# RWKV-7 and gMLP trunk: k, r, v and g projections by single channel tiles, with hi and lo activations side by side in one 512-column product

## The chip, the cores and the metric

The kernel runs on one core of a Trainium2 chip. The metric is device microseconds for one execution; smaller is better. A core has a matrix engine (TensorE, PE in the profile), three engines that work on tiles (VectorE is DVE, ScalarE is ACT, GpSimd is POOL), and SyncE (SP), which here issues most DMA transfers.

## The reference

Two residual layers over 256 tokens of width 2048, then a final RMS norm. All inputs are float32. Layer 0, where the change lies, projects the normalised input `z` to 4 x 4096 channels (r, k, v and a gate g) and to four low-rank inputs:

```python
def rwkv7_bidir_mixer(h, w_in, mu_prev, mu_next, ...):
    z = h @ w_in
    zs, gate = z[..., :SHIFT_COLS], z[..., SHIFT_COLS:]
    zs = zs + mu_prev * (shift_prev(zs) - zs) + mu_next * (shift_next(zs) - zs)
    r, k, v, dw, da = jnp.split(zs, ...)
    ...                                   # decay, in-context rate, normalised keys kk
    for d, rev in ((0, False), (1, True)):
        y = y + wkv_scan(rh, heads(decay), kd_h, vh, -kk, kk * a_h, rev)
        bonus = bonus + jnp.sum(rh * kd_h * r_k, axis=-1, keepdims=True) * vh
    ...                                   # group norm of y, plus bonus
    return (out * jax.nn.silu(gate)) @ w_out
```

Layer 1 is a gated gMLP: `u`, `v` and a gate from one projection to 3 x 4096 channels, a 128 x 128 spatial mixing per group of 256 channels, and an output projection.

## The kernel before

**Precision by halves.** Weights and activations are float32; each operand is split into hi (rounded to the matmul's fp32r form) and lo (the remainder), and a product is hi·hi + hi·lo + lo·hi. Weights arrive as raw tiles of 128 x 1024 floats (512 KB, two buffers, issued by SP). ACT casts raw to hi (L150) and DVE subtracts to get lo (L151); up to three converted tiles wait ahead of PE (three buffers each of hi and lo). The activations `z` are stored transposed as `zh` and `zl`, 128 channels by 16 k tiles by 256 tokens each.

**The mixer stage.** The 4096 channels are 32 channel tiles of 128, handled as 16 pairs (b). A pass p projects k and r of pair p and v and g of pair p-1, in four segments. A segment (`mains`, L436) fetches four weight tiles of 4 k tiles x 256 columns. For every k tile and each of the two channel tiles, `project` issues three matmuls through `mm3` (L165 to L167), each with 256 moving columns: whi·zh, whi·zl, wlo·zh. Both channel tiles accumulate in the two halves of one PSUM bank (tag "acc", two buffers). Then k, r and v pass through `shifted` (ACT scales by c0, DVE adds the neighbour tokens' shares, all read from PSUM: L395, L396, L398), and g through a tanh and one DVE operation (L450, L451).

**The second layer already has another form.** `project_wide` (L194) works on an interleaved tile `zc` with hi and lo side by side: whi times the 512 columns of hi and lo fills both halves of a bank (L204), wlo times the 256 hi columns adds to the first half (L206). `gated` then copies the second half to SBUF on ACT (L1065) and adds the first half on DVE (L1066).

**What sets the order.** Beside the projections a pass runs, for earlier pairs: low-rank updates (`rates`, tile `up`), the factors of the recurrence (`factors`), gram matrices (`grams`, tile `gp`, masked into `Gs`), a triangular inverse on DVE (`inverses`, L637 and L639, 31 steps), transposes (`bp`, `vp`), the chunk chain (`chain`, tiles `xp`, `uu`, `sp`, `yp`) and `finish`. Each is a generator that yields a due time within a planned pass of `PERIOD` = 78 units; a loop always advances the one that is due first. `mains` yields after each k tile. From this program a scheduler with a simulated timeline lays down each engine's fixed instruction order and the semaphores. Engines execute their own order strictly.

The storage of `zh` and `zl` is used again later for activations of the output projections (`oA` in `early_out`, `pA` in the second layer).

Of the kernel before, what the change touches and what calls it, by code (L numbers as in the profile page):

```python
# [22 lines left out]
def trunk(tc, x, norm_g, final_norm_g, w_in, mu_prev, mu_next, w0, w_up, a0, a_up, k_k, k_a, r_k,  # L23
# [149 lines left out]
    def want_cols(w, c_off, b, name):  # L173
        a = min(KT, 1 << int(math.log2(RAW // b)))
        wv = w.rearrange("(k p) c -> p k c", p=P)
        for k0 in range(0, KT, a):
            want(wv[:, k0:k0 + a, c_off:c_off + b], a, b, f"{name}{k0}")
# [32 lines left out]

    def acc_pair(name):
        return sm(name, "acc").rearrange("p (i t) -> p i t", i=2)
# [69 lines left out]
    zT = (zp.tile([P, KT, T], F32R, tag="zh", name="zh"), zp.tile([P, KT, T], F32R, tag="zl", name="zl"))  # L282
# [73 lines left out]
    for todo in plan:  # L356
        for s, b in todo:
# [3 lines left out]
            else:  # L361
                want_cols(w_in, segment[s] + b * 2 * P, 2 * P, f"w{s}{b}_")
# [27 lines left out]
    def shifted(acc, dst, b, m):  # L390

        for cl in range(2):
            a = acc[:, cl]
            j = m * NCT + 2 * b + cl
            S.activation(dst[:, cl], a, AF.Identity, scale=c0[:, j:j + 1])  # L395
            V.scalar_tensor_tensor(dst[:, cl, 1:], a[:, :T - 1], col["mp"][:, j:j + 1], dst[:, cl, 1:],  # L396
                                   ALU.mult, ALU.add)
            V.scalar_tensor_tensor(dst[:, cl, :T - 1], a[:, 1:], col["mn"][:, j:j + 1], dst[:, cl, :T - 1],  # L398
                                   ALU.mult, ALU.add)
# [36 lines left out]
    def mains(todo, st):  # L436
        slot = dict(k=0, r=4, g=12, v=8) if "k" in dict(todo) else dict(v=0, g=4)
        last = -4
        for s, b in todo:
# [5 lines left out]
            acc = acc_pair(f"acc{s}{b}")  # L445
            for i, _ in enumerate(project(2 * P, [acc[:, 0], acc[:, 1]], zT)):
                yield last * MT + i * dt
            if s == "g":
                SG = fr.tile([P, 2, T], F32, tag="SG", name=f"SG{b}", bufs=2)
                S.activation(SG, acc, AF.Tanh, scale=0.5)  # L450
                V.scalar_tensor_tensor(SG, SG, 1.0, acc, ALU.add, ALU.mult)  # L451
                st[b]["SG"] = SG
            elif s == "v":
                Vt = fr.tile([P, 2, T], F32, tag="Vt", name=f"Vt{b}", bufs=2)
                shifted(acc, Vt, b, 2)
                st[b]["Vt"] = Vt
            else:
                t = fr.tile([P, 2, T], F32, tag=f"{s}t", name=f"{s}t{b}")
                shifted(acc, t, b, dict(r=0, k=1)[s])
# [711 lines left out]
```

## Time and profile before

| | us |
|---|---|
| median of 3 runs | 2230.92 (2229.87 to 2234.58) |
| the profiled execution's own time | 2229.16 |
| its span, first to last instruction | 2227.4 |
| the mixer stage in it (37.9 to 1273.9) | 1236.0 |
| PE busy in the span | 2179.0 |
| DVE busy in the span | 1608.1 |
| ACT busy in the span | 1345.2 |

The span is 1.8 us shorter than the profiled execution's time. Busy time of PE is a union of overlapping matmuls: it tells that PE has work, and not how fast it works. The mean length of one matmul in a row (for example 290 ns) is longer than the distance to the next matmul's start for the same reason. A row that ends in "idle before, releaser" tells how long the engine stood still ahead of such instructions, and which instruction ended the wait.

### The profile page before, as it was taken

To read this page: it belongs to the slowest core of one execution; us is meant where nothing else is said; L and a number is where in the kernel's file an instruction comes from. 1 tells how busy PE (TensorE), PEld (TensorE's weight loads), DVE (VectorE), ACT (ScalarE), POOL (GpSimd) and SP (SyncE) were. 2 spreads that over 40 slices of the span, in tenths; PEclk is the share of its full clock that TensorE was granted. 3 is DMA by queue.
4 is the path that set the end of the run, shared out by engine and by line. 5 is a ranking of instruction groups with operands and counts; after the bars stand their busy time and mean duration, and the time that the engine had idled before them with its cause. 6 is when DMAs were issued, how large, how long until landed. Compare 5 with 4: busy or idle time off the path is not lost.

```text
span 2227.4 us, 48630 instructions
## 1 busy us (share of the span) xinstructions
PE 2179.0 (98%) x19984; PEld 1944.7 (87%) x19984; DVE 1608.1 (72%) x3121; ACT 1345.2 (60%) x2128; POOL 171.8 (8%) x230
## 2 busy tenths in 40 slices
PE   7999999999999999999999999999999999999998
PEld 7889999999999999999999877778888888888886
DVE  5797788787977977887888764465546777777444
ACT  6556777777767676776767664464444444444443
POOL 2210110011001101100010000000000000000000
PEclk9999999999999999999999999999999999999999
DMA  5555444454445544444545555586766666665664
GB/s 167 140 145 142 109 126 134 125 137 112 130 127 143 139 126 131 129 125 136 137 124 138 167 174 177 173 263 189 221 204 190 198 189 195 195 193 192 195 198 154
DMA packets 352687, 356.01 MB, mean 160 GB/s; under 512 B 78160, under 2 KB 300112, under 8 KB 352336
## 3 DMA queue, kind: packets, MB, share of 16 engines
q1 hardware_dynamic: 332208, 331.66, 51.6%
q10 hardware_dynamic: 20256, 21.24, 3.2%
q8 instruction: 157, 2.57, 0.5%
q14 instruction: 66, 0.54, 0.1%
HBM read 329.78 MB, written 6.29 MB: 151 GB/s over the span
## 4 chain that ended last, share of the span: by engine, by line
PE 69%; ACT 10%; DMA 9%; DVE 8%; issue 3%; ACTq 0%; SPq 0%; POOL 0%; POOLq 0%; DVEq 0%
PE uacc L204 5%; PE gacc L204 5%; DMA raw_o<-in_rwkv_w_out_dram 3%; PE oacc L166 3%; PE oacc L167 3%; PE oacc L165 3%; PE gp L584 3%; PE gacc L206 3%; PE uacc L206 3%; PE vacc L167 3%; PE vacc L165 3%; PE vacc L166 3%; ACT Dt L623 2%; PE accv L165 2%; PE accg L167 2%
## 5 line engine op out<-in xcount | busy, mean ns | idle before, releaser
L204 PE MATMUL uacc<-z,whi_u 128*128 128x512 f32 x512 | 179.0, 394 | 0.0
L204 PE MATMUL gacc<-z,whi_g 128*128 128x512 f32 x512 | 177.3, 393 | 0.0
L167 PE MATMUL accg<-zh,wlo_wg 128*128 128x256 f32 x512 | 149.6, 292 | 2.5 <-DVE wlo_wg L151 2.4
L165 PE MATMUL accv<-zh,whi_wv 128*128 128x256 f32 x512 | 149.2, 291 | 1.1 <-ACT whi_wv L150 1.1
L167 PE MATMUL accr<-zh,wlo_wr 128*128 128x256 f32 x512 | 148.7, 290 | 0.6 <-DVE wlo_wr L151 0.5
L165 PE MATMUL acck<-zh,whi_wk 128*128 128x256 f32 x512 | 148.1, 289 | 1.1 <-ACT whi_wk L150 1.1
L165 PE MATMUL accr<-zh,whi_wr 128*128 128x256 f32 x512 | 149.0, 291 | 0.0
L165 PE MATMUL accg<-zh,whi_wg 128*128 128x256 f32 x512 | 148.4, 290 | 0.0
L166 PE MATMUL accr<-zl,whi_wr 128*128 128x256 f32 x512 | 148.1, 289 | 0.0
L167 PE MATMUL accv<-zh,wlo_wv 128*128 128x256 f32 x512 | 147.5, 288 | 0.1
L167 PE MATMUL acck<-zh,wlo_wk 128*128 128x256 f32 x512 | 146.2, 286 | 1.0 <-DVE wlo_wk L151 1.0
L166 PE MATMUL accv<-zl,whi_wv 128*128 128x256 f32 x512 | 147.2, 287 | 0.0
L166 PE MATMUL accg<-zl,whi_wg 128*128 128x256 f32 x512 | 147.0, 287 | 0.0
L166 PE MATMUL acck<-zl,whi_wk 128*128 128x256 f32 x512 | 147.0, 287 | 0.0
L206 PE MATMUL uacc<-z,wlo_u 128*128 128x256 f32 x512 | 142.4, 284 | 0.0
L206 PE MATMUL gacc<-z,wlo_g 128*128 128x256 f32 x512 | 140.2, 279 | 0.0
L151 DVE TENSOR_TENSOR wlo_v<-raw_v,whi_v 128x1024 fp32r<-128x1024 f32 x64 | 78.4, 1225 | 80.4 <-ACT whi_v L150 80.4
L151 DVE TENSOR_TENSOR wlo_o<-raw_o,whi_o 128x1024 fp32r<-128x1024 f32 x64 | 78.2, 1224 | 77.5 <-ACT whi_o L150 77.2
L639 DVE TENSOR_TENSOR X<-X,TD 128x126 f32<-128x126 f32 (+22 forms) x496 | 126.5, 255 | 9.4
L637 DVE TENSOR_TENSOR TD<-La,X 128x126 f32<-128x126 f32 (+22 forms) x496 | 125.6, 253 | 10.6
L151 DVE TENSOR_TENSOR wlo_p<-raw_p,whi_p 128x1024 fp32r<-128x1024 f32 x60 | 73.9, 1232 | 75.7 <-ACT whi_p L150 75.7
L150 ACT CAST whi_p<-raw_p 128x1024 fp32r<-128x1024 f32 x60 | 63.1, 1051 | 91.5 <-PE oacc L167 87.3
(331 smaller groups left out, 6842.3 us busy)
## 6 DMA issues: line engine op xcount, KB each, us to landing
raw_wk<-in_rwkv_w_in_dram SPq DMA_DIRECT2D x64, 512.0 KB, 3.7
raw_wr<-in_rwkv_w_in_dram SPq DMA_DIRECT2D x64, 512.0 KB, 3.7
raw_wv<-in_rwkv_w_in_dram SPq DMA_DIRECT2D x64, 512.0 KB, 3.7
raw_wg<-in_rwkv_w_in_dram SPq DMA_DIRECT2D x64, 512.0 KB, 3.7
raw_o<-in_rwkv_w_out_dram SPq DMA_DIRECT2D x64, 512.0 KB, 4.0
raw_v<-in_gmlp_w_in_dram SPq DMA_DIRECT2D x64, 512.0 KB, 3.7
raw_u<-in_gmlp_w_in_dram SPq DMA_DIRECT2D x64, 512.0 KB, 3.5
raw_g<-in_gmlp_w_in_dram SPq DMA_DIRECT2D x64, 512.0 KB, 3.6
```

Of the source, the lines that this page charges most:

```text
L150: latest[0] = S.copy(hi, raw)
L151: latest[1] = V.tensor_tensor(lo, raw, hi.bitcast(F32), ALU.subtract)
L165: PE.matmul(acc, a[0], b[0], start=first, stop=False, skip_group_check=True)
L166: PE.matmul(acc, a[0], b[1], start=False, stop=False, skip_group_check=True)
L167: PE.matmul(acc, a[1], b[0], start=False, stop=last, skip_group_check=True)
L204: PE.matmul(acc.rearrange("p h t -> p (h t)"), hi[:, j, cs], zc[:, k].rearrange("p h t -> p (h t)"), start=k == 0, stop=False, skip_group_ ...
L206: PE.matmul(acc[:, 0], lo[:, j, cs], zc[:, k, 0], start=False, stop=k == KT - 1, skip_group_check=True)
L584: PE.matmul(gp[h][:, c].rearrange("p q t -> p (q t)"), BK[H[h], d, cl, c].rearrange("p q t -> p (q t)"), AR[H[h], d, cl, c].rearrange("p q ...
L623: S.copy(Dt[r0:r0 + 32].rearrange("p t u -> p u t"), Gs[q * 32:q * 32 + 32, h, :, q * 32:q * 32 + 32])
L637: V.tensor_tensor(tv, La[:, j, 0:j].unsqueeze(2).to_broadcast([P, j, n]), X[:, j:j + 1, m:].to_broadcast([P, j, n]), ALU.mult)
L639: V.tensor_tensor(X[:, 0:j, m:], X[:, 0:j, m:], tv, ALU.add)
```

## The change

The k, r, v and g projections take the second layer's form, one channel tile at a time. A weight tile is now 8 k tiles x 128 columns, so that every contiguous run in memory is 512 bytes instead of 1024, with 512 KB per load as before. `mains` calls `project_wide` for each of the two channel tiles of a segment with a PSUM bank of its own: per k tile one matmul of 512 columns and one of 256. It yields after each k tile of one channel tile, twice as often as before. The eviction copies the lo half to a temporary `pa` (ACT), adds the hi half (DVE), and the shifting or gating reads `pa` instead of PSUM, per channel tile. `zh` and `zl` become two strided views of one interleaved tile, and the later users of that storage get one tile in place of two.

```diff
     def want_cols(w, c_off, b, name):
-        a = min(KT, 1 << int(math.log2(RAW // b)))
+        a = min(KT, RAW // b if b == P else 1 << int(math.log2(RAW // b)))
...
-    zT = (zp.tile([P, KT, T], F32R, tag="zh", name="zh"), zp.tile([P, KT, T], F32R, tag="zl", name="zl"))
+    zi = zp.tile([P, KT, 2, T], F32R, tag="z", name="z0")
+    zT = [zi[:, :, i] for i in range(2)]
...
-                want_cols(w_in, segment[s] + b * 2 * P, 2 * P, f"w{s}{b}_")
+                for cl in range(2):
+                    want_cols(w_in, segment[s] + (2 * b + cl) * P, P, f"w{s}{b}_{cl}")
...
-    def shifted(acc, dst, b, m):
-
-        for cl in range(2):
-            a = acc[:, cl]
-            j = m * NCT + 2 * b + cl
-            S.activation(dst[:, cl], a, AF.Identity, scale=c0[:, j:j + 1])
-            V.scalar_tensor_tensor(dst[:, cl, 1:], a[:, :T - 1], col["mp"][:, j:j + 1], dst[:, cl, 1:],
-                                   ALU.mult, ALU.add)
-            V.scalar_tensor_tensor(dst[:, cl, :T - 1], a[:, 1:], col["mn"][:, j:j + 1], dst[:, cl, :T - 1],
-                                   ALU.mult, ALU.add)
+    def shifted(a, dst, j):
+
+        S.activation(dst, a, AF.Identity, scale=c0[:, j:j + 1])
+        V.scalar_tensor_tensor(dst[:, 1:], a[:, :T - 1], col["mp"][:, j:j + 1], dst[:, 1:], ALU.mult, ALU.add)
+        V.scalar_tensor_tensor(dst[:, :T - 1], a[:, 1:], col["mn"][:, j:j + 1], dst[:, :T - 1], ALU.mult, ALU.add)
...
-            acc = acc_pair(f"acc{s}{b}")
-            for i, _ in enumerate(project(2 * P, [acc[:, 0], acc[:, 1]], zT)):
-                yield last * MT + i * dt
-            if s == "g":
-                SG = fr.tile([P, 2, T], F32, tag="SG", name=f"SG{b}", bufs=2)
-                S.activation(SG, acc, AF.Tanh, scale=0.5)
-                V.scalar_tensor_tensor(SG, SG, 1.0, acc, ALU.add, ALU.mult)
...
+            tag, n = dict(k=("kt", 1), r=("rt", 1), v=("Vt", 2), g=("SG", 2))[s]
+            dst = fr.tile([P, 2, T], F32, tag=tag, name=f"{tag}{b}", bufs=n)
+            for cl in range(2):
+                acc = sm(f"acc{s}{b}_{cl}", "acc").rearrange("p (h t) -> p h t", h=2)
+                for i, _ in enumerate(project_wide(P, [acc], zi)):
+                    yield last * MT + (cl * KT + i) * dt / 2
+
+                a = fr.tile([P, T], F32, tag="pa", name=f"pa{s}{b}_{cl}")
+                S.copy(a, acc[:, 1])
+                V.tensor_tensor(a, acc[:, 0], a, ALU.add)
+                if s == "g":
+                    S.activation(dst[:, cl], a, AF.Tanh, scale=0.5)
+                    V.scalar_tensor_tensor(dst[:, cl], dst[:, cl], 1.0, a, ALU.add, ALU.mult)
+                else:
+                    shifted(a, dst[:, cl], dict(r=0, k=1, v=2)[s] * NCT + 2 * b + cl)
+            st[b][dict(r="Rt", k="Kt", v="Vt", g="SG")[s]] = dst
...
-        oA = [zp.tile([P, HE, T], F32R, tag=t, name=f"{t}_o0") for t in ("zh", "zl")]
+        oA = zp.tile([P, 2, HE, T], F32R, tag="z", name="z_o0")
+        oA = [oA[:, i] for i in range(2)]
...
-    pA = [zp.tile([P, HE, T], F32R, tag=t, name=f"{t}_o1") for t in ("zh", "zl")]
+    pA = zp.tile([P, 2, HE, T], F32R, tag="z", name="z_o1")
+    pA = [pA[:, i] for i in range(2)]
```

More of the change, by code (lines that the diff above doesn't have):

```diff
@@ L209, in project_wide @@
                 yield
-    def acc_pair(name):
-        return sm(name, "acc").rearrange("p (i t) -> p i t", i=2)
     n3 = 3 * NCT
@@ L444, in mains @@
             yield last * MT
-            acc = acc_pair(f"acc{s}{b}")
-            for i, _ in enumerate(project(2 * P, [acc[:, 0], acc[:, 1]], zT)):
-                yield last * MT + i * dt
-            if s == "g":
-                SG = fr.tile([P, 2, T], F32, tag="SG", name=f"SG{b}", bufs=2)
[L450 to L459, printed above, removed]
-                st[b][dict(r="Rt", k="Kt")[s]] = t
+            tag, n = dict(k=("kt", 1), r=("rt", 1), v=("Vt", 2), g=("SG", 2))[s]
[13 more added lines that the diff above has]
+            st[b][dict(r="Rt", k="Kt", v="Vt", g="SG")[s]] = dst
         if ("g", NB - 1) in todo:
```

## The prediction

> **What bounds the kernel now.** I read the page's engine line first, then its chain, then the stretch in which the four projections run.
>
> ```profile
> PE 2179.0 (98%) x19984; PEld 1944.7 (87%) x19984; DVE 1608.1 (72%) x3121; ACT 1345.2 (60%) x2128; POOL 171.8 (8%) x230
> PE 69%; ACT 10%; DMA 9%; DVE 8%; issue 3%; ACTq 0%; SPq 0%; POOL 0%; POOLq 0%; DVEq 0%
> ```
>
> The matrix engine (PE) works 98% of the span, and the chain that ended last runs through it for 69%. The other 31% says that ACT, DVE and the weight loads are never far behind. By stretch (columns: PE, weight load, DVE, ACT, POOL, each with its instructions; clock, DMA share, GB/s):
>
> ```profile
> 37.90:1273.90 1236.00, 1215.05 (x14578) 1135.07 (x14576) 1013.90 (x2321) 868.87 (x1489) 133.37 (x170) 0.99 0.49 133
> 220.00:1260.00 1040.00, 1031.64 (x12844) 959.69 (x12839) 854.86 (x2015) 749.05 (x1297) 104.83 (x136) 1.00 0.49 131
> 794.00:848.90 54.90, 54.76 (x666) 50.98 (x665) 50.41 (x133) 36.34 (x67) 4.02 (x7) 1.00 0.46 126
> ```
>
> The first row is the mixer stage, from the first k product to the last g product; all that changes lies in it. The second is its steady part: PE idles 1040 - 1031.64 = 8.4 us, the granted clock is 1.00, DVE is busy 82%, ACT 72%. So PE sets the pace there. The third row is the crowded part of one pass over a channel pair: DVE is busy 50.41 of 54.90 us (92%).
>
> A busy PE tells nothing of its rate, since matmuls overlap. The rate comes from start to start in the timeline: an unbroken run of k and r products, first and last start, 39 spacings apart; and an unbroken run of the u and g products of the second layer, which already have the form that the change brings, 20 pairs apart (columns: start, us of one, engine, line).
>
> ```profile
> 787.23 0.28 PE L166 MATMUL acck<-zl,whi_wk 128*128 128x256 f32 x1
> ...
> 791.90 0.28 PE L166 MATMUL accr<-zl,whi_wr 128*128 128x256 f32 x1
> ...
> 1749.87 0.39 PE L204 MATMUL uacc<-z,whi_u 128*128 128x512 f32 x1
> 1750.10 0.28 PE L206 MATMUL uacc<-z,wlo_u 128*128 128x256 f32 x1
> ...
> 1756.80 0.39 PE L204 MATMUL gacc<-z,whi_g 128*128 128x512 f32 x1
> ```
>
> One 256-column matmul takes 4.67 / 39 = 0.1197 us, so the three products of one weight tile (hi by hi, hi by lo, lo by hi) take 0.3592 us. The pair of one 512-column and one 256-column matmul takes 6.93 / 20 = 0.3465 us.
>
> **The change part by part.** *The products.* Four segments of 32 channel tiles with 16 k tiles each are 2048 places. Each loses three matmuls of 256 columns and gets one of 512 and one of 256: 0.3592 - 0.3465 = 0.0127 us less, 2048 x 0.0127 = 26.0 us off the path. The rounding of the four starts to 0.01 us allows 2.6 us either way. The columns are the same in number (768); what goes is the overhead of the third matmul.
>
> The Trainium skill ("TensorE: Matmul & The Clock Gate", Back-to-back issue gap) gives for isolated matmuls the columns at the full clock and about 2.5 ns on top. By it, 3 x 109.2 would become 215.8 + 109.2 ns, and 2048 x 2.5 ns are only 5.1 us, an estimate from that page. The two runs above measure 119.7 ns where it has 109.2 and 346.5 where it has 325.0, so the trace has a larger price per matmul, and the measurement decides.
>
> *Cuts.* The run of projections is cut where other products come in. What a cut costs:
>
> ```profile
> 701.40 0.49 PE L584 MATMUL gp<-AR,BK 64*128 64x128 f32 x4
> ...
> 705.91 0.28 PE L165 MATMUL acck<-zh,whi_wk 128*128 128x256 f32 x1
> 706.12 0.69 PE L722 MATMUL uu<-Xs,TTs 128*64 128x64 f32 x16
> 706.74 1.16 PE L584 MATMUL gp<-AR,BK 64*128 64x128 f32 x16
> 707.83 0.39 PE L166 MATMUL acck<-zl,whi_wk 128*128 128x256 f32 x1
> 708.05 0.28 PE L167 MATMUL acck<-zh,wlo_wk 128*128 128x256 f32 x1
> ...
> 710.05 0.69 PE L729 MATMUL sp<-SUV,BT 128*64 128x64 f32 x16
> ...
> 1282.22 0.39 PE L167 MATMUL oacc<-whi_o,rt_o 128*128 128x512 f32 x1
> 1282.54 0.38 PE L713 MATMUL xp<-SUV,Gs 128*64 128x64 f32 x4
> ...
> 1769.29 0.40 PE L204 MATMUL uacc<-z,whi_u 128*128 128x512 f32 x1
> 1769.52 0.38 PE L1095 MATMUL sgu<-wsT,vn_bh 128*128 128x128 f32 x2
> ```
>
> The last matmul before the cut takes 0.21 instead of 0.12, the first behind it 0.22: 0.19 us a cut. A 512-column matmul ahead of a cut takes 0.32 in one row and 0.23 in another, so the price stays about the same. The program hands the projections out in steps half as long, so two kinds of work that shared a cut can now fall into two. The stretch around 706 has such a cut, with uu and gp together. The other cuts nearby begin at 701.40 and 710.05, so there is one about every 4 us and some 300 in the stage. Bounds: no more cuts, or a third more (100 x 0.19 = 19 us). I take 20 more, 4 us, nearer to none since the order of the other work stays.
>
> *Evictions.* Each of the 128 channel tiles gets an ACT copy and a DVE addition, which the second layer already does at the same shape; g's tanh and its product become two of 256 columns instead of one of 512.
>
> ```profile
> L1065 ACT COPY Gt<-uacc 128x256 f32<-128x256 f32 x32 | 12.0, 374 | 16.8 <-PE uacc L206 16.8
> L1066 DVE TENSOR_TENSOR U<-uacc,Gt 128x256 f32<-128x256 f32 x32 | 13.5, 421 | 2.1 <-ACT Gt L1065 0.7
> L450 ACT ACTIVATE SG<-accg 128x512 f32<-128x512 f32 x16 | 9.7, 607 | 0.1
> L481 ACT ACTIVATE TH<-up,pc 128x256 f32<-128x256 f32 x64 | 26.9, 473 | 8.6 <-PE up L167 7.8
> L451 DVE SCALAR_TENSOR_TENSOR SG<-SG,accg 128x512 f32<-128x512 f32 x16 | 10.9, 682 | 9.0 <-ACT SG L450 9.0
> L568 DVE SCALAR_TENSOR_TENSOR BQ<-rt,pc,TH 128x256 f32<-128x256 f32 x32 | 14.1, 469 | 0.0
> L395 ACT ACTIVATE rt<-accr,c 128x256 f32<-128x256 f32 x32 | 15.2, 474 | 12.1 <-DVE rt L398 11.6 <-PE accr L167 0.2
> L396 DVE SCALAR_TENSOR_TENSOR rt<-accr,pc,rt 128x255 f32<-128x255 f32 x32 | 15.3, 479 | 2.6 <-ACT rt L395 2.1
> ```
>
> ACT gets 128 x 0.374 + 16 x (2 x 0.473 - 0.607) = 53.3 us, DVE 128 x 0.421 + 16 x (2 x 0.469 - 0.682) = 58.0 us. The shifting operations now read SBUF instead of PSUM; the 469 ns of L568, whose operands all lie in SBUF, against the 479 of L396 say that this saves nothing worth counting. None of the added time lies on PE's path as long as DVE and ACT keep up: in the stage DVE idles 1236 - 1013.9 = 222.1 us now and 1210 - 1071.9 = 138.1 then (89% busy), ACT 367 now and 288 then. If that cover were gone, all 58 us would be paid. What the cover lets through I size by the steady row: PE idles 8.4 us there while DVE has its present room; with the room down by 222.1 / 138.1 = 1.61 I let the idle grow alike, by 5 us. Bounds: nothing, or 58 us.
>
> The new temporary has one buffer. One tile's eviction is 0.374 + 0.421 + 0.474 + 2 x 0.479 = 2.2 us against 16 x 0.3465 = 5.5 us to fill the next, so it holds nobody up. A new handoff comes with it: on ACT the scaling of a tile queues behind DVE's addition, and behind it wait weight casts. In exchange a handoff goes: L395 waits 11.6 us for L398 in the row above, the second tile's scaling for the first tile's shifts out of the same bank. I set the two equal. A bank is held 0.8 us then, and comes round every 5.5 us.
>
> *Weight loads.* Each load still brings 512 KB but in runs of 512 bytes, 1024 instead of 512. No load of that shape is in the trace; the nearest have 1024 runs of 256 bytes.
>
> ```profile
> raw_wk<-in_rwkv_w_in_dram SPq DMA_DIRECT2D x64, 512.0 KB, 3.7
> RC<-AR SPq DMA_DIRECT2D x32, 256.0 KB, 5.2
> Gs<-AR SPq DMA_DIRECT2D x32, 256.0 KB, 3.7
> L145 SPq DMA_DIRECT2D raw_wk<-in_rwkv_w_in_dram x64: 367/368/1567, 31.1 to 1165.0; - x64
> L684 SPq DMA_DIRECT2D RC<-AR x32: 596/663/1619, 85.5 to 1294.4; - x32
> L150 ACT CAST whi_wk<-raw_wk 128x1024 fp32r<-128x1024 f32 x64 | 67.2, 1051 | 65.7 <-DMA raw_wk<-in_rwkv_w_in_dram 43.4 <-PE accg L166 12.5 <-PE acck L166 5.3
> ACT whi_wk L150 <- DMA raw_wk<-in_rwkv_w_in_dram: 43.4, 21, 5.9
> L151 DVE TENSOR_TENSOR wlo_wk<-raw_wk,whi_wk 128x1024 fp32r<-128x1024 f32 x64 | 78.0, 1220 | 35.2 <-ACT whi_wk L150 34.9 <-PE xp L713 0.2
> ```
>
> Landing is thus between 3.7 and 5.2 us; I take 4.4, the middle, with issue on SP's queue at 0.66 instead of 0.37. The dependent copies of RC and Gs stand on the same queue and go up to 0.3 us later per load. A raw buffer then turns in 0.66 + 4.4 + 1.05 + 1.22 = 7.3 us, and two give a load every 3.7 us; the stage asks for 256 + 16 loads in 1210 us, one every 4.4, with three converted ahead. So the longer landing is hidden behind the converted tiles and costs nothing; if that cover is thin it comes back as the second rival. Bounds of its cost: 0, and what that rival gives.
>
> *At no cost.* The grouping rule of the loads gives 8 k tiles for a 128-column load by the old and the new formula. The hi and lo activations move into one tile of the same bytes, so no instruction is added; the later users of that storage write after the last g product as before.
>
> **The sum.** Against the profiled execution: 2229.16 - 26.0 + 4 + 5 = 2212.2 us. That execution lies 1.76 us below the median of the runs, 2230.92, so the median should be 2213.9; I say 2213.
>
> **The rivals.**
> *DVE takes over as the bound (slower).* Place: the crowded part of a pass (794 to 849), with 4.5 us of DVE idle per pass. Five of a pass's eight additions should fall there, 2.1 us, and the extra handoffs eat more. It decides once PE, three weight tiles ahead, runs out of them. For it: 92% busy there. Against it: PE's waits in the steady part are on ACT, and on DVE there is one of 0.2 us:
>
> ```profile
> PE yp L731 <- ACT SUV L724: 2.8, 4, 1.1
> ...
> PE up L165 <- DVE NK L503: 0.2, 1, 0.2
> ```
>
> If half of the 58 us gets through: 2230.9 - 26 + 4 + 29 = 2238; all of it: 2267.
> *The weight supply falls behind.* For it: ACT already sits waiting for landings, 43.4 us at 21 of the 64 loads of wk. Against it: the 3.7 against 4.4 us above. If a third of the 256 loads is awaited, as wk's are now, each 0.7 us late, 60 us reach ACT; if a third of that gets to PE, 20 us: 2213.9 + 20 = 2234; none, 2214.
> *The isolated rate holds and only 5 us come off.* As a mechanism here: the third matmul's overhead is hidden by the others. 2230.9 - 5 + 9 = 2235. Against it: the two unbroken runs above.
> *No cuts and waits are added and the 512-column matmul hides part of the price of a cut.* For it the 0.23 at 1769.29, against it the 0.32 at 1282.22. 2230.9 - 26 - 150 x 0.09 = 2191, without the last term 2205; so about 2198.
>
> **How the numbers follow.** No change means within 0.2%, 2226.5 to 2235.4; that is about what a measurement of this kernel can tell. Forecast 0.57, at 2203 to 2222; DVE takes over 0.14 (slower); the supply 0.15, of it 0.08 faster and 0.07 same; the isolated rate 0.06 (same); the last 0.08 (faster). Faster 0.73, same 0.13, slower 0.14. The range leaves out most of the DVE case, and the lowest part of the last: 2196 to 2239.
>
> **What would show it.** The spacing of the projections should be 0.23 and 0.12 in turn, 4096 matmuls of k, r, v and g instead of 6144; the stage some 17 us shorter; DVE at 88 to 89% in it and PE's idle in the steady part 10 to 15 us; landings of 4 to 5 us. It would be wrong if PE waits on lo weights, on Gs or on BK for more than 20 us in all, if the pair takes more than 0.352 us, or if the projections are cut much oftener than 300 times.

## The result, and the profile after

The changed kernel takes 2289.69 us (median of 4 runs, 2287.49 to 2294.89), the kernel before on the same chip 2232.52 us (median of 4). The ratio is 1.026, with a 95% interval of 1.0238 to 1.0282: 57 us slower. The prediction said 2213 us, 2196 to 2239, and was wrong in sign.

The page of the changed kernel: busy time by engine, the chain that ended last by engine, and the load of the k weights.

```profile
PE 2194.6 (96%) x17936; PEld 1849.3 (81%) x17936; DVE 1651.5 (72%) x3265; ACT 1387.1 (61%) x2272; POOL 183.2 (8%) x230
PE 62%; DVE 15%; ACT 10%; DMA 9%; issue 4%; POOL 1%; ACTq 0%; POOLq 0%; DVEq 0%; SPq 0%
raw_wk<-in_rwkv_w_in_dram SPq DMA_DIRECT2D x64, 512.0 KB, 3.9
```

PE has 2048 matmuls fewer, as the change says, and yet is busy 15.6 us longer. DVE's part of the chain went from 8% to 15%, PE's from 69% to 62%. A load of wk in 512-byte runs lands in 3.9 us here, where the prediction estimated 4.4 and the longer runs took 3.7.

All of the time lies before the second layer. This is its first weight load on PE (the row gives count, shortest/median/longest in ns, first and last start), before and then after:

```profile
L204 PEld LDWEIGHTS uacc<-z,whi_u x512: 187/187/192, 1672.4 to 2030.5; 128*128 128x128 f32 x171
```

```profile
L204 PEld LDWEIGHTS uacc<-z,whi_u x512: 187/187/192, 1732.7 to 2090.9; 128*128 128x128 f32 x171
```

The second layer starts 60.3 us later, and the spans differ by 60.5 (2227.4 and 2287.9). From that start to the end both kernels take 555 us. By stretch, in the changed kernel (columns as in the prediction), the mixer stage and its steady part:

```profile
37.00:1324.70 1287.70, 1226.81 (x12445) 1035.00 (x12444) 1049.97 (x2441) 909.36 (x1627) 144.57 (x170) 0.96 0.48 127
220.00:1260.00 1040.00, 1000.69 (x10662) 842.80 (x10660) 850.71 (x2027) 749.10 (x1356) 106.53 (x130) 0.97 0.48 125
```

The stage went from 1236.0 to 1287.7 us. PE idles 60.9 us in it where it idled 21.0, and the granted clock is 0.96 instead of 0.99. In the steady part PE idles 39.3 us, not 8.4. DVE is the row to look at: it was busy 854.86 of 1040 us before and is busy 850.71 now, though it has more to do. Its share did not rise to fill the idle time. The work was stretched to the share that it already had.

The products did become shorter. The timeline shows an unbroken run of g's products, first and last start, 16 pairs apart:

```profile
1260.18 0.40 PE L204 MATMUL accg<-z,whi_wg 128*128 128x512 f32 x1
...
1265.74 0.39 PE L204 MATMUL accg<-z,whi_wg 128*128 128x512 f32 x1
```

5.56 / 16 = 0.3475 us a pair, against 0.3465 predicted. What PE now waits for (total, times, longest in us):

```profile
PE gp L578 <- DVE Gs L583: 17.1, 10, 4.7
...
PE accv L204 <- ACT whi_wv L150: 5.3, 5, 1.7
PE accg L206 <- DVE wlo_wg L151: 5.1, 2, 4.3
PE vp L667 <- ACT TTs L654: 4.8, 4, 2.4
PE accv L206 <- DVE wlo_wv L151: 4.4, 10, 0.9
...
PE acck L206 <- DVE wlo_wk L151: 1.8, 2, 1.0
```

In the kernel before, the wait for Gs, which empties the banks of the gp products, was this:

```profile
PE gp L584 <- DVE Gs L589: 1.7, 1, 1.7
```

Three groups of the eviction in the changed kernel (busy, mean ns of one, idle before and its releaser):

```profile
L448 DVE TENSOR_TENSOR par<-accr,par 128x256 f32<-128x256 f32 x32 | 13.3, 417 | 11.5 <-ACT par L447 11.5
L391 ACT ACTIVATE rt<-par,c 128x256 f32<-128x256 f32 x32 | 16.3, 510 | 14.3 <-DVE par L448 14.0
L447 ACT COPY par<-accr 128x256 f32<-128x256 f32 x32 | 11.8, 368 | 1.9 <-DVE n L489 1.8
```

The durations are those of the second layer's rows that the prediction used. The idle columns are new: for r alone DVE stands 11.5 us for the copies and ACT 14.0 us for the additions.

One stall can be followed row by row, in the timeline of the changed kernel (start, us, engine, and in brackets the idle time before, with its releaser):

```profile
639.78 1.03 ACT L150 CAST whi_wr<-raw_wr 128x1024 fp32r<-128x1024 f32 x1
...
643.61 0.39 DVE L448 TENSOR_TENSOR pak<-acck,pak 128x256 f32<-128x256 f32 x1
643.92 2.35 DVE L151 TENSOR_TENSOR wlo_wr<-raw_wr,whi_wr 128x1024 fp32r<-128x1024 f32 x2
...
645.19 0.33 SPq L143 DMA_DIRECT2D raw_wu<-in_rwkv_w_up_dram  x1
...
650.31 1.04 ACT L150 CAST whi_wu<-raw_wu 96x1024 fp32r<-96x1024 f32 x1 [5.76 <-DMA raw_wu<-in_rwkv_a_up_dram]
651.38 1.22 DVE L151 TENSOR_TENSOR wlo_wu<-raw_wu,whi_wu 96x1024 fp32r<-96x1024 f32 x1 [2.11 <-ACT whi_wu L150]
651.71 1.79 PE L770 MATMUL yt<-ident,yn 128*64 128x64 f32 x24 [1.79 <-ACT yn L760]
652.72 1.11 DVE L636 STREAM_TRANSPOSE TD<-X 128x512 f32<-128x512 f32 x1
...
654.64 0.58 PE L645 MATMUL qp<-Tn,NQ 32*32 32x32 f32 x14 [1.14 <-DVE Tn L637]
```

The cast of a raw buffer ends at 640.8, but DVE is behind with other work, the new addition at 643.61 among it (0.39 us of the 3.1 us between), and subtracts only at 643.92. The buffer comes free then, so the next load is issued at 645.19. ACT idles 5.76 us for it. The operations behind that cast on ACT are late too, and PE waits 1.79 us for one of them (`yn`). DVE stands 2.11 us behind ACT, and so the transposes of the inverse are late and PE waits 1.14 us for them. The next stretches show what follows:

```profile
640.00:650.00 10.00, 9.87 (x72) 8.22 (x70) 8.71 (x29) 2.75 (x4) 4.03 (x2) 1.00 0.48 140
650.00:660.00 10.00, 7.16 (x109) 6.05 (x110) 6.61 (x11) 9.57 (x20) 0.45 (x1) 0.71 0.39 110
660.00:670.00 10.00, 10.00 (x114) 8.52 (x114) 6.09 (x11) 6.05 (x10) 2.59 (x3) 0.78 0.26 79
```

PE idles 2.8 us between 650 and 660. In the ten us after that it is busy throughout, at a clock of 0.78. DVE, which was 87% busy when it fell behind, is then 61 to 66% busy. This is how an engine has idle time on average and none when it is needed.

### The profile page after: what moved, and what is told of

Read it like the earlier page. It is cut to its first block, busy times and chain, and to the rows that moved or that the text cites. A ratio compares the mean times of both kernels' runs of the same rounds, so it can differ in the third digit from the quotient of the medians.

```text
span 2287.9 us, 44963 instructions
## 1 busy us (share of the span) xinstructions
PE 2194.6 (96%) x17936; PEld 1849.3 (81%) x17936; DVE 1651.5 (72%) x3265; ACT 1387.1 (61%) x2272; POOL 183.2 (8%) x230
## 4 chain that ended last, share of the span: by engine, by line
PE 62%; DVE 15%; ACT 10%; DMA 9%; issue 4%; POOL 1%; ACTq 0%; POOLq 0%; DVEq 0%; SPq 0%
PE uacc L204 5%; PE gacc L204 5%; PE oacc L166 4%; PE oacc L167 3%; PE oacc L165 3%; PE accg L204 3%; PE uacc L206 3%; PE gacc L206 3%; PE vacc L165 3%; PE vacc L166 3%; PE vacc L167 3%; PE accv L204 2%; DMA raw_wk<-in_rwkv_w_in_dram 2%; PE gp L578 2%; PE accr L204 2%
## 5 line engine op out<-in xcount | busy, mean ns | idle before, releaser
L204 PE MATMUL accr<-z,whi_wr 128*128 128x512 f32 x512 | 202.3, 428 | 1.8 <-DVE pak L448 1.7
L204 PE MATMUL accv<-z,whi_wv 128*128 128x512 f32 x512 | 191.2, 407 | 5.5 <-ACT whi_wv L150 5.3
L204 PE MATMUL accg<-z,whi_wg 128*128 128x512 f32 x512 | 187.5, 404 | 0.0
L204 PE MATMUL acck<-z,whi_wk 128*128 128x512 f32 x512 | 185.1, 400 | 1.9 <-ACT whi_wk L150 1.9
L206 PE MATMUL accv<-z,wlo_wv 128*128 128x256 f32 x512 | 149.8, 293 | 4.6 <-DVE wlo_wv L151 4.4
L206 PE MATMUL accg<-z,wlo_wg 128*128 128x256 f32 x512 | 148.5, 290 | 5.1 <-DVE wlo_wg L151 5.1
L206 PE MATMUL accr<-z,wlo_wr 128*128 128x256 f32 x512 | 152.7, 298 | 0.2
L206 PE MATMUL acck<-z,wlo_wk 128*128 128x256 f32 x512 | 148.1, 289 | 1.8 <-DVE wlo_wk L151 1.8
L578 PE MATMUL gp<-AR,BK 64*128 64x128 f32 x1024 | 109.1, 308 | 17.2 <-DVE Gs L583 17.1
L204 PEld LDWEIGHTS accr<-z,whi_wr 128*128 128x128 f32 x512 | 102.9, 201 | 26.2 <-DVE pak L448 2.0
```

The costliest lines, as they stand in the source:

```text
L204: PE.matmul(acc.rearrange("p h t -> p (h t)"), hi[:, j, cs], zc[:, k].rearrange("p h t -> p (h t)"), start=k == 0, stop=False, skip_group_ ...
L206: PE.matmul(acc[:, 0], lo[:, j, cs], zc[:, k, 0], start=False, stop=k == KT - 1, skip_group_check=True)
L578: PE.matmul(gp[h][:, c].rearrange("p q t -> p (q t)"), BK[H[h], d, cl, c].rearrange("p q t -> p (q t)"), AR[H[h], d, cl, c].rearrange("p q ...
```

## The experiments

Eighteen kernels ran, and all are in the table. Ratio and interval are against the kernel before on the same chip. "Stage" runs from the first k product to the last g product. "DVE" is its busy time in the stage and the share of it, "products" the time that PE is busy with the matmuls of k, r, v and g, "rest" the stage less that (other matmuls and idle time). "Second layer" is the start of its first weight load on PE. All are from one profiled execution, in us. Kernels that were measured beside the same runs of before are compared by their times; where others are compared, the difference of their ratios is taken times 2232 us, since the time of before differs by up to 7 us between such groups of runs.

| kernel | us | ratio (95%) | stage | DVE | products | rest | second layer |
|---|---|---|---|---|---|---|---|
| before | 2232.52 | 1 | 1235.8 | 1013.7, 82% | 843.9 | 391.9 | 1672.4 |
| after | 2289.69 | 1.026 (1.0238–1.0282) | 1287.7 | 1050.0, 82% | 825.8 | 461.9 | 1732.7 |
| e1_no_halves_sum | 2241.91 | 1.0074 (1.0044–1.0103) | 1238.3 | 1008.7, 81% | 808.7 | 429.6 | 1684.9 |
| e2_pair_loads | 2340.7 | 1.0518 (1.0487–1.0548) | 1343.4 | 1064.5, 79% | 835.7 | 507.7 | 1782.0 |
| e3_tile_loads_alone | 2238.14 | 1.0051 (1.0026–1.0076) | 1255.2 | 1015.3, 81% | 850.1 | 405.1 | 1681.8 |
| e4_evictions_alone | 2253.28 | 1.0125 (1.0095–1.0154) | 1257.5 | 1050.5, 84% | 853.7 | 403.8 | 1696.2 |
| e7_two_products | 2255.12 | 1.0135 (1.0094–1.0176) | 1210.8 | 980.6, 81% | 615.6 | 595.2 | 1698.3 |
| e8_before_plan_74 | 2215.79 | 0.9964 (0.9944–0.9984) | 1225.0 | 1015.8, 83% | 850.3 | 374.7 | 1656.5 |
| e9_after_plan_74 | 2245.78 | 1.0113 (1.0054–1.0172) | 1245.9 | 1046.9, 84% | 813.8 | 432.1 | 1687.5 |
| e10_sum_on_gpsimd | 2279.19 | 1.0243 (1.0192–1.0294) | 1276.7 | 1053.5, 83% | 825.0 | 451.7 | 1725.0 |
| e11_third_raw_buffer | 2263.19 | 1.0141 (1.0108–1.0175) | 1263.9 | 1049.8, 83% | 819.7 | 444.2 | 1708.0 |
| e12_after_plan_70 | 2269.28 | 1.0169 (1.0135–1.0202) | 1266.9 | 1047.8, 83% | 820.2 | 446.7 | 1714.0 |
| e13_before_third_raw_buffer | 2210.04 | 0.9903 (0.9871–0.9935) | 1224.6 | 1012.2, 83% | 849.0 | 375.6 | 1651.5 |
| e14_two_products_third_raw | 2210.68 | 0.9906 (0.987–0.9942) | 1190.2 | 992.3, 83% | 590.6 | 599.6 | 1651.4 |
| e15_no_halves_sum_third_raw | 2221.81 | 0.9947 (0.9932–0.9962) | 1224.2 | 1007.9, 82% | 799.3 | 424.9 | 1664.8 |
| e17_after_plan_74_third_raw | 2243.3 | 1.008 (1.0064–1.0097) | 1249.2 | 1046.8, 84% | 813.1 | 436.1 | 1689.8 |
| e18_before_plan_74_third_raw | 2197.24 | 0.9877 (0.9862–0.9892) | 1211.6 | 1017.0, 84% | 844.2 | 367.4 | 1641.0 |
| e19_two_products_half_inverse | 2103.75 | 0.9429 (0.9381–0.9477) | 1091.3 | 894.0, 82% | 592.2 | 499.0 | 1543.4 |
| e20_after_half_inverse | 2216.31 | 0.9927 (0.9893–0.9961) | 1228.4 | 961.3, 78% | 817.7 | 410.7 | 1659.9 |
| e21_before_half_inverse | 2198.03 | 0.9852 (0.9815–0.9888) | 1213.2 | 930.4, 77% | 843.1 | 370.1 | 1642.2 |

### One part of the change at a time

**e1_no_halves_sum**: the changed kernel without the copy and the addition; the shifts read the hi half in PSUM, so the hi by lo half is left out of the sum.

```diff
-                a = fr.tile([P, T], F32, tag="pa", name=f"pa{s}{b}_{cl}")
-                S.copy(a, acc[:, 1])
-                V.tensor_tensor(a, acc[:, 0], a, ALU.add)
+                a = acc[:, 0]
```

> The changed kernel without the two added eviction operations: shifting and gating read the first half of the bank in PSUM, so the hi weights by lo activations half is computed and left out of the sum. Theory A (the copy and the addition, and the handoffs they put into the fixed orders of ACT and DVE, make DVE late): the rate gain of 26 us appears, 2200 to 2215 us. Theory B (512-byte weight runs and loads by single channel tile starve PE): stays at 2275 to 2290. Theory C (the plan handed out in steps half as long gives a worse fixed order): stays at 2270 to 2290.

The ratio goes from 1.026 to 1.0074: 41 us of the 57 go with the copies and additions, and the second layer starts 48 us earlier. But the kernel is still not faster than before, although it has the shorter products, and so it lies between the ranges expected: the rate gain of theory A does not appear.

**e2_pair_loads**: the changed kernel with the loads, and the plan's steps, of the kernel before; both channel tiles in one run of products with two banks.

```diff
-                for cl in range(2):
-                    want_cols(w_in, segment[s] + (2 * b + cl) * P, P, f"w{s}{b}_{cl}")
+                want_cols(w_in, segment[s] + b * 2 * P, 2 * P, f"w{s}{b}_")
...
+            accs = [sm(f"acc{s}{b}_{cl}", "acc").rearrange("p (h t) -> p h t", h=2) for cl in range(2)]
+            for i, _ in enumerate(project_wide(2 * P, accs, zi)):
+                yield last * MT + i * dt
             for cl in range(2):
-                acc = sm(f"acc{s}{b}_{cl}", "acc").rearrange("p (h t) -> p h t", h=2)
-                for i, _ in enumerate(project_wide(P, [acc], zi)):
-                    yield last * MT + (cl * KT + i) * dt / 2
+                acc = accs[cl]
```

> The changed kernel with the loads of before (4 k tiles by 256 columns, 1024-byte runs), both channel tiles filled together in two banks, one plan step per k tile as before; wide products and evictions as changed. Theory A: 2275 to 2300, the evictions are all there and now come two at a time. Theory B: 2205 to 2220. Theory C: 2205 to 2225.

2340.7 us, slower than the change itself and above every expected range. It holds both banks until both tiles are evicted, and PE waits for that:

```profile
PE accr L204 <- DVE pak L447: 16.2, 12, 3.5
```

So it brought a wait of its own and can't tell what the loads cost; e3 can.

**e3_tile_loads_alone**: the loads, the order and the plan's steps of the change, but three products of 256 columns, evicted from PSUM as before.

```diff
-                for i, _ in enumerate(project_wide(P, [acc], zi)):
+                for i, _ in enumerate(project(P, [acc[:, 0]], zT)):
...
+                a = acc[:, 0]
```

> The loads, the order by single channel tile and the finer plan steps of the changed kernel, with the three 256-column products of before, evicted from PSUM without copy or addition. Theory A: within 0.5% of before, 2225 to 2242. Theory B: 2270 or more, and landings awaited on ACT. Theory C: 2270 or more.

2238.14 us, 12 us above the 2226.33 of before measured beside it. Beside e1 this is the first surprise: e1 differs from e3 only in the products, which take 41 us less in it (808.7 against 850.1), and yet e1 is not faster (4 us slower, inside the uncertainty of the two). Its rest is 25 us longer, and its second layer starts 3 us later.

**e4_evictions_alone**: the kernel before with a copy on ACT and one more operation of the addition's size on DVE (a maximum) for every channel tile, and g gated per tile.

```diff
+    def evicted(acc, b, m, cl):
+        a = fr.tile([P, T], F32, tag="pa", name=f"pa{m}_{b}_{cl}")
+        S.copy(a, acc[:, cl])
+        V.tensor_tensor(a, acc[:, cl], a, ALU.max)
+        return a
```

> The kernel before with the two eviction operations added for every channel tile (copy of the sum to a temporary on ACT, and on DVE the maximum of the sum and its copy, which is the sum), and g by two tiles. Theory A: the loss without the rate gain, 2290 to 2315. Theories B and C: 2231 to 2245, since DVE still idles a tenth of the stage.

2253.28 us, 27 us above before. With the products untouched, the evictions alone cost 27 us, where the prediction had allowed 5. This lies between the expected ranges. Each DVE operation came with a copy on ACT, so the run does not tell which of the two engines makes the loss. The steady row:

```profile
220.00:1260.00 1040.00, 1022.63 (x12536) 948.50 (x12536) 872.46 (x2107) 758.56 (x1379) 112.72 (x134) 0.99 0.46 127
```

### Is PE the bound at all?

**e7_two_products**: the kernel before without the hi by lo product of the four projections. This leaves out 2048 matmuls of 256 columns, some 245 us of PE's time at 0.1197 us each.

```diff
+                    if two:
+                        PE.matmul(acc, hi[:, j, cs], zT[0][:, k], start=k == 0 and i % 2 == 0, stop=False,
+                                  skip_group_check=True)
+                        PE.matmul(acc, lo[:, j, cs], zT[0][:, k], start=False, stop=k == KT - 1,
+                                  skip_group_check=True)
+                        continue
```

> The kernel before with the hi weights by lo activations product of the four projections left out: 2048 matmuls of 0.1197 us, 245 us of PE's work, fewer; everything else as before. Theory P (PE alone sets the pace of the mixer stage, as the prediction had it): 1985 to 2010 us. Theory D (DVE, ACT and the weight loads in their fixed orders run level with PE, so PE time taken off is not time off): 2120 to 2200, with PE idle in the stage.

2255.12 us: slower than before by 30 us, with a third of the projections' matmuls gone, and above both expected ranges. In the stage the products take 228 us less and the rest 203 us more. Of these 203 us, 113 are idle time of PE, and 91 are the other matmuls, which take longer at a granted clock of 0.89 instead of 0.99. The chain and the steady row:

```profile
PE 46%; DVE 18%; ACT 16%; DMA 15%; issue 4%; SPq 0%; POOL 0%; ACTq 0%; POOLq 0%; DVEq 0%
...
220.00:1260.00 1040.00, 930.87 (x10973) 845.79 (x10973) 847.54 (x1993) 729.19 (x1272) 110.71 (x134) 0.89 0.47 130
```

PE is busy 90% of the steady part and idles 109 us. DVE is about where it was, at 847.54 us after 854.86.

The plan's own cost for a pass was tried too, since a plan made for one PE load may suit another badly: **e8_before_plan_74** and **e9_after_plan_74** (`PERIOD` 74 instead of 78), and later **e12_after_plan_70**.

```diff
-    PERIOD, CT, TBT, TEO = 78.0, 13.0, 37.0, 1.2
+    PERIOD, CT, TBT, TEO = 74.0, 13.0, 37.0, 1.2
```

> The kernel before with one number of the plan changed, PERIOD 74 instead of 78: another fixed order of the same instructions. It sizes what a mere change of order is worth. If order is worth little: within 0.3% of before, 2220 to 2234. If it is worth as much as the 12 us that loads and order by single tiles cost alone: 1% either way or more.

> The changed kernel with PERIOD 74 instead of 78. If the loss is a bad order of the same work: 2230 to 2265. If it is the added work and handoffs: within 1% of the changed kernel, 2270 to 2310.

2215.79 us for the one, 9 us below before. The other's ratio is 1.0113, 33 us below the change as it stands. That lies in the range expected if a bad order made the loss, so a part of the 57 us belongs to the plan. But the change still loses under the same plan, by 30 us. The order written out is itself worth 0.4% in the one kernel and 1.5% in the other, so a single pair of kernels can't separate parts of up to some 33 us.

**e10_sum_on_gpsimd**: the changed kernel, with ACT copying both halves and GpSimd adding them, so that DVE has no addition.

```diff
-                S.copy(a, acc[:, 1])
-                V.tensor_tensor(a, acc[:, 0], a, ALU.add)
+                S.copy(both, acc)
+                a = both[:, 0]
+                G.tensor_tensor(a, a, both[:, 1], ALU.add)
```

> The changed kernel with the addition of the halves moved from DVE to GpSimd: ACT copies all 512 columns to SBUF, GpSimd adds. DVE has about as much work as before. If DVE's added work (54 us) makes the loss: 2240 to 2260, near the 2242 of the run without the sum. If the handoffs do, with one more engine in the row of the eviction: 2280 or more.

The ratio is 1.0243, only 4 us below the change as it stands and at the edge of what was expected of the handoffs. The groups show why DVE was not relieved: its two inverse steps in the changed kernel, then in this one, and the new addition.

```profile
L633 DVE TENSOR_TENSOR X<-X,TD 128x126 f32<-128x126 f32 (+22 forms) x496 | 125.9, 254 | 8.9
...
L631 DVE TENSOR_TENSOR TD<-La,X 128x126 f32<-128x126 f32 (+22 forms) x496 | 124.7, 251 | 9.8
```

```profile
L634 DVE TENSOR_TENSOR X<-X,TD 128x126 f32<-128x126 f32 (+22 forms) x496 | 146.2, 295 | 9.9
...
L632 DVE TENSOR_TENSOR TD<-La,X 128x126 f32<-128x126 f32 (+22 forms) x496 | 138.6, 279 | 10.8
...
L449 POOL TENSOR_TENSOR par<-par 128x256 f32<-128x256 f32 x32 | 32.8, 1024 | 190.4 <-ACT par L447 175.3 <-DVE Gs L584 15.1
```

An addition takes 1.02 us on GpSimd, and DVE's own small operations got longer: 295 ns instead of 254, and 279 instead of 251 for TD, together 34 us. DVE lost 53 us of additions, but its busy time in the stage went from 1050.0 to 1053.5. The run says nothing against DVE as the bound; it took no work from it.

### A third raw buffer

The stall above went through the two raw weight buffers. **e11_third_raw_buffer** and **e13_before_third_raw_buffer** give the changed kernel and the kernel before a third one; **e14_two_products_third_raw** does so for e7.

```diff
-        return raw_pools[0].tile([P, RAW], F32, tag="raw", name=f"raw_{name}", bufs=2)
+        return raw_pools[0].tile([P, RAW], F32, tag="raw", name=f"raw_{name}", bufs=3 if raw_pools[0] is wp else 2)
```

> The changed kernel with three buffers instead of two for the raw weights. Theory S (DVE, late by the evictions, frees the two raw buffers late; the next load starts late, ACT and DVE then stand at the head of their queues for it, and PE idles): most of the loss comes back, 2225 to 2250. Theory E (the eviction's handoffs delay the other work directly, with no part of the weight supply): 2275 to 2295.

> The changed kernel with PERIOD 70, after 78 (2290 us) and 74 (2246 us). If the plan places the projections too late for the faster products: 2215 to 2240. If 74 was a lucky draw among orders: 2250 to 2290.

> The kernel before with three raw buffers, as the control: PE idles 8 us in its steady part, so by either theory 2215 to 2232.

> The kernel with the third product left out (245 us less of PE's work, which ran at 2255 us) and with three raw buffers. Theory S: the weight ring was what held it, so it falls well under the kernel before, 2130 to 2200. Theory E, or DVE's serial work as the bound: 2230 to 2260.

The ring of two buffers costs every form some time: 27 us in the changed kernel (ratio 1.0141), 22 in the one before (0.9903), 51 in e7 (from 1.0135 to 0.9906). It explains little of the loss: with three buffers in both kernels the change still costs 53 of the 57 us. None of e11, e13 and e14 lies in a range that was expected: e11 and e14 fall between those of the two theories, e13 is 5 us below its own. e12's ratio of 1.0169 lies between those of `PERIOD` 78 and 74, so the plan's cost has no steady effect.

The pair e13 and e14 is the test on which the explanation rests. Both have three buffers, and e14 has 2048 matmuls less. The start of the second layer and the steady part, e13 first:

```profile
L204 PEld LDWEIGHTS uacc<-z,whi_u x512: 187/187/192, 1651.5 to 2009.7; 128*128 128x128 f32 x171
...
220.00:1260.00 1040.00, 1036.70 (x12848) 963.53 (x12847) 858.52 (x2032) 750.83 (x1302) 106.17 (x136) 1.00 0.49 132
```

```profile
L210 PEld LDWEIGHTS uacc<-z,whi_u x512: 187/187/192, 1651.4 to 2009.6; 128*128 128x128 f32 x171
...
220.00:1260.00 1040.00, 946.91 (x11215) 860.13 (x11212) 862.54 (x2032) 748.11 (x1310) 99.55 (x136) 0.88 0.49 132
```

The second layers start 0.1 us apart with 258 us of products less (849.0 and 590.6), and DVE is busy 862.54 us in e14's steady part after 858.52. (The last g product does end 35 us earlier; the passes behind it do not.) PE's busy time in the stage falls by less than the products do, by 146 us (1216.4 to 1070.0): PE idles 112 us more, the granted clock is 0.89 instead of 1.00, and the other matmuls take 112 us longer. Leaving out a third of the projections' matmuls is worth nothing here, so there is little reason for 26 us off their rate to be worth 26. How much of the gain the lower clock takes back is not shown.

### Work taken from DVE

DVE's largest single piece of work in the stage is the 31-step inverse, X and TD, some 250 us in the rows above. Leaving out every second step (15 of 31; the inverse is then not the full one) takes 119 us of it away in e19: the two rows sum to 131.4 us there, and to 250.6 in e14.

```diff
-        for j in range(31, 0, -1):
+        for j in range(31, 0, -2):
```

> The kernel with the third product left out and three raw buffers (2211 us), with the same inverse steps left out. PE has 245 us less work than before and DVE 126 us less. Theory V: 2080 to 2140. If neither PE nor DVE's work sets it: 2190 to 2215.

> The changed kernel with every second of the 31 steps of the triangular inverse left out: about 126 us of DVE's 1050 in the stage gone, from a serial part of each pass, and nothing else. Theory V (DVE's work and the handoffs around it in each pass hold the stage): the loss goes and the rate gain shows, 2195 to 2220. If the weight ring or the order holds it: 2255 to 2290.

> The control: the kernel before with the same steps left out. Theory V, with PE and DVE level in the kernel before: little or nothing to gain while PE is busy 99%, 2210 to 2230.

> The changed kernel without the copy and the addition of the halves (2242 us) and with three raw buffers. DVE's work is that of the kernel before. Theory V with the two engines level: no better than the kernel before with three raw buffers (2210 us), 2205 to 2225. If the weight ring alone had eaten the rate gain: 2180 to 2195.

e14 becomes 107 us faster (e19, with three buffers too, 2103.75 us). That is almost all of what DVE lost: its busy time up to the second layer's start falls by 111 us (1248.6 to 1138.0), where 2048 matmuls had brought nothing. The inverse is also one step in the row of dependent work of each pass (grams, inverse, transposes, chain), and the stage's clock rose from 0.89 to 0.93 with it. So the run shows that the passes set the time, and not whether DVE's load or the length of that row does it. The changed kernel becomes 74 us faster (e20), the kernel before 33 us (e21). In e21's steady row PE idles only 3 us of 1040, which fits PE as the bound once DVE is relieved, though a busy PE alone does not show it:

```profile
220.00:1260.00 1040.00, 1036.89 (x13063) 970.71 (x13065) 799.70 (x1654) 752.78 (x1310) 108.94 (x134) 1.00 0.51 136
```

With DVE relieved the change should now show its 26 us. The control e21 already says that it doesn't: it fell 12 us below its expected range, while e20 came out within its own. PE's busy time with the products of k, r, v and g (one row each), in e21 and then in e20, both at a clock of 0.99:

```profile
38.20:1251.40 1213.20, 202.74 (x1536) 0.99 0.51 135
38.20:1251.40 1213.20, 215.77 (x1536) 0.99 0.51 135
38.20:1251.40 1213.20, 213.98 (x1536) 0.99 0.51 135
38.20:1251.40 1213.20, 210.65 (x1536) 0.99 0.51 135
```

```profile
37.80:1266.20 1228.40, 197.92 (x1024) 0.99 0.51 134
37.80:1266.20 1228.40, 208.28 (x1024) 0.99 0.51 134
37.80:1266.20 1228.40, 201.74 (x1024) 0.99 0.51 134
37.80:1266.20 1228.40, 209.78 (x1023) 0.99 0.51 134
```

They sum to 843.1 and 817.7: 25.4 us less, near the predicted 26. That it comes so near is partly luck: in the other pairs of the old and the new products the difference is between 18 us (before and after) and 50 (e13 and e15). The total is 18 us more all the same (2198.03 and 2216.31), because the rest of the stage is 41 us longer. PE idles 20.5 us instead of 12.9 in it; the other 33 us are the other matmuls', of nearly the same number (8506 and 8477). e15, the change without its additions and with three buffers, gives the same from another side: 10 us behind e13, with products 50 us shorter and a rest 49 us longer.

### The best of both

> The changed kernel with PERIOD 74 and three raw buffers. If the two gains (44 and 27 us) add up: 2215 to 2225, level with the kernel before. If they take the same waits away: 2235 to 2250. Theory V: above the next kernel in any case.

> The kernel before with PERIOD 74 and three raw buffers (9 and 22 us alone). PE is busy 99% of its steady part, so what is left to gain is small: 2198 to 2212, the fastest so far.

Both edits together (plan at 74, three raw buffers) on the changed kernel (e17) give 2243.3 us, on the kernel before (e18) 2197.24 us, a ratio of 0.9877 (0.9862 to 0.9892). e18 is faster than both kernels of this case, and it has the old form of the projections. Under equal settings the change costs 57 us as it was made, 53 with three buffers, 30 with plan 74 and 46 with both.

## Why the prediction was wrong

**The step that failed is "None of the added time lies on PE's path as long as DVE and ACT keep up", with DVE's 222 us of idle time in the stage as the cover.** It priced 58 us of work added to DVE at 5 us, by scaling PE's idle time with DVE's idle time. The runs show that this idle time was not room: the evictions cost 27 us added to the kernel before (e4), and 41 and 43 us come back when they are left out of the changed kernel (e1; e15 beside e11). In every kernel that has the whole inverse DVE is busy 79 to 84% of the stage, whatever PE has to do. When PE lost 258 us of products DVE's share stayed and the time with it (e13, e14); when DVE lost 111 us of busy time the total fell by 107 (e19). Much of the remaining fifth is waiting for other engines. In the trace of before DVE waits 90 us for casts of these projections' weights and 44 us for the ACT copies ahead of the inverse; in the changed kernel it also waits for ACT's half of an eviction, 11.5 us for r in the row above. That every new instruction on DVE brings such waits along fits these rows, but it is argued and not shown.

Afterwards a sum of the right size can be made. DVE's rows rise by 4 x 13.3 us for the additions and 2.5 for g's product, 56 us. Its busy time, where overlapping instructions count once, rises by 43 in the span and by 36 in the stage (1013.7 to 1050.0). 36 us at a share of 0.82 are 44 us of stage, 56 in full are 56; measured are 51.9, and 60 to the second layer's start. It is fitted to the result and no rule: in e4 DVE's busy time in the stage rose by 37 us too, and the total by 27.

Point by point:

- *The products, -26.0 us.* The rate was right and the place wrong. The pair takes 0.3475 us, which makes the term 24 us instead of 26, and the products shrink by 25.4 us under equal clocks (e20, e21), by 18 to 50 in other pairs. But they were not on the path that sets the end, so none of it comes off. Of three comparisons of shorter against longer products one ends level (e1 and e3) and two 10 and 18 us on the wrong side (e15 and e13, e20 and e21).
- *"PE sets the pace there."* This is the reading behind it, from 8.4 us of idle in 1040 and a clock of 1.00. PE and the passes were almost level: less work for PE alone brings nothing (e14 beside e13), and half the inverse left out alone, 120 us of DVE's rows, brings 33 (e21). The order on PE puts projections where it would otherwise wait for the passes, so PE is busy whichever of the two is the bound. e14 shows that the passes alone take as long.
- *Evictions and waits, +5 us.* They cost 27 us on the kernel before (e4) and in the change 41 with two buffers (e1) and 43 with three (e15 against e11). The middle between the bounds of 0 and 58, and more, would have been the right size.
- *Loads, 0 us.* The landing was shorter than estimated, 3.9 against 4.4 us. Loads, order and plan steps together cost 12 us (e3). The hidden part was not the landing but the buffers: ACT's waits for loads of wk, 43.4 us in 21 times before, are 73.3 us in 47 times in the row of after that follows this list, and a third buffer brings 27 us. The 7.3 us for a buffer's turn counted no waiting in the orders of ACT and DVE, and in the stall above the subtraction starts 3.1 us after its cast has ended. But a third buffer brings 22 us in the kernel before too, so the supply makes only some 4 us of the difference.
- *Cuts, +4 us.* Counted in the timelines, the projections are cut into 291 runs instead of 383: fewer, not more. No loss came from here.
- *The rivals.* The nearest one was "DVE takes over as the bound", at 0.14 and 2238 to 2267. It was still too low, since it kept the -26. Without that credit and with all 58 us paid it gives 2230.9 + 58 = 2289, close to the measured time; that the two agree so well is partly luck, as the parts below don't add up. The isolated rate and the hidden cut are refuted by the pair's 0.3475 us and by the sign; the weight supply is a small part of the loss, 4 us by the third buffer.
- *The signs named in advance.* Waits of PE on Gs and on lo weights were to be under 20 us: they are 17.1 and 11.3, 28.4 together. DVE was to rise to 88 to 89% of the stage: it is at 82%. Both told the failure directly.

The row for the loads, from the waits of the changed kernel (total, times, longest in us):

```profile
ACT whi_wk L150 <- DMA raw_wk<-in_rwkv_w_in_dram: 73.3, 47, 3.7
```

Open: how the 57 us divide. Parts tried alone (27 for the evictions, 12 for the loads and order) give 39; the additions taken out of the change give 41, and leave 16. Another plan alone takes the loss from 57 to 30 us, so these parts are not known better than that. Whether DVE's load, the copies on ACT (a copy for every addition) or the length of the dependent row in a pass makes an eviction dear was not separated either, and e14 ran with the plan of 78 alone. Where the 33 us go by which the other products of e20 take longer than e21's was not traced. Whether the lower clock costs anything beyond the idle time that precedes it could not be tried apart from it.

## What to carry to other kernels

An in-order engine that is busy 80% of a stage can be part of what bounds it: its idle time is then waiting between handoffs, and no room for new work. Here 53 us of additions on VectorE, each with a copy on ScalarE, cost 27 to 43 us. Before you make the busiest engine faster, leave a large piece of its work out and see whether the time moves; here a third of the projections' matmuls was worth nothing, and 111 us of VectorE's busy time 107 us once those matmuls were gone. When two engines are almost level, a change that moves work from the one to the other must be priced on both.

## What the runs showed of the hardware

Short idle times of PE went with a lower clock there and afterwards. In the changed kernel 2.8 us of idle between 650 and 660 go with a clock of 0.71 there and 0.78 in the next ten us, in which PE is busy throughout. In e14, with waits of up to 2.0 us, a stretch of ten us ran at half the clock with PE always busy (PE is the third number, the clock the third from the end):

```profile
610.00:620.00 10.00, 6.71 (x90) 4.55 (x90) 9.59 (x29) 6.27 (x14) 0.82 (x3) 0.89 0.44 99
620.00:630.00 10.00, 8.32 (x43) 7.45 (x43) 9.93 (x35) 3.79 (x12) 2.23 (x2) 0.50 0.01 2
630.00:640.00 10.00, 10.00 (x113) 9.21 (x115) 6.36 (x16) 7.80 (x13) 1.64 (x1) 0.50 0.08 27
```

The Trainium skill ("TensorE: Matmul & The Clock Gate", Part 1: The HAM clock gate) has a clock of either half or full speed, half after an idle window of some 3.4 us. The 0.50 agrees with that, and 0.71 and 0.78 can be means over both; that such a drop follows less than 3 us of idle, in waits of under 2 us each, is what the rows of the changed kernel add.

GpSimd is no free adder beside VectorE: 128 x 256 took it 1.02 us against 0.42, and VectorE's inverse steps became 11 to 16% longer in that kernel (e10). The Trainium skill ("GPSIMD Engine Reference", Specifications) says that the two contend for SBUF when VectorE has two inputs there, as these steps have; the rows agree. Weight loads of 512 KB in runs of 1024 bytes landed in 3.7 us in the kernel before. In runs of 512 bytes they took 3.9 us in the changed kernel, but 3.6 to 3.7 in e3, which has the same loads, so no cost of the shorter runs is shown.
